# A hybrid decoder trunk on one core: the opening with another transfer order, engines in written order, and the second token half by feature tile

## The chip, the cores and the metric

One core of a Trainium2 chip runs the whole kernel in one launch. The metric is the device time in microseconds (us) of one execution, as the median of several. The core has five instruction queues that run beside each other, each in its own order: TensorE (PE, matmuls and transposes; its weight loads are shown apart as PEld), VectorE (DVE), ScalarE (ACT), GpSimd (POOL) and SyncE (SP, which here only issues transfers). Sixteen DMA engines move the data.

## What is computed

One layer with d = 1024 and 1024 tokens, all in float32. Only the opening and what feeds from it matter here:

```
mod = silu(c) @ ada_w + ada_b;  shift, scale, gate = split(mod, 3)
h = rms_norm(x, norm_w) * (1 + scale) + shift
proj = h @ w_in            # 10 slices: hq hf hi hz | gq gk gv gz ga | mg
y_h = hgrn2_branch(hq, hf, hi, hz);  y_g = gla_branch(gq, gk, gv, gz, ga)
merged = sigmoid(mg[0]) * (y_h @ w_branch[0]) + sigmoid(mg[1]) * (y_g @ w_branch[1])
out = rms_norm(x + gate * (merged @ w_out), final_norm_w)
```

Both branches are gated linear recurrences over the tokens, done in chunks ("attention" below).

## The kernel before

Features lie on the partitions: h is held as eight feature tiles of 128 rows by 1024 tokens. Each float32 operand of a large product is split into a rounded part hi and a rest lo, and a product is three matmuls: hi by hi, lo by hi and hi by lo. `split` does that: ACT casts hi (L192), DVE or POOL subtracts (L195).

The opening makes h and, with it, the first group of projections: six column tiles of w_in (gq, and half of gk; `NG = 6`), for each of two token halves of 512. Its steps, with their lines:

- `load_x` (L137) brings four token tiles of x, `norm_x` squares and sums them on ACT (L203), takes the root (L205) and scales on DVE (L206, L207). `transpose_x` turns 128 columns of four token tiles on PE (L214), and ACT copies the result out (L216).
- `load_mod` (L235) brings the shift and scale columns of ada_w for a block of one or two feature tiles, from all eight k tiles. `make_mod` weights and adds the k tiles on DVE (L246 the first, L250 the others), PE adds over the partitions with a column of ones (L258), DVE writes modv and amul (L260, L262). For block 0 the first four k tiles went through PE instead (L256). The blocks are `[(0, 1), (1, 1), (2, 2), (4, 2), (6, 2)]`: first tile, count.
- `make_h` applies modulation on ACT (L223), splits the result, and POOL stores h to memory (L226).
- `load_wg` (L280) brings 128 rows of w_in into one of three parts of the buffer xb, and `prep_wg` splits them, with POOL for lo.
- The products of the first half (L348) run feature tile by feature tile into six half banks, `accs`. `make_ga` (L304) makes the gate's low rank input, `qk_out` (L294, L296) copies the six results out.
- The second half: all eight tiles of h are made in a row, and `first_group` (L371) then goes column tile by column tile, each over all eight feature tiles, into new banks.

A small allocator, `Slots`, hands out 46 slots of 4 KB a partition, first freed first used; a new tile waits for all readers of the slot's last one. There are two banks for small PSUM tiles (`mtile`), taken in turn. Up to L323 (`order.close()`) PE, ACT and DVE keep the order of the program; behind it a list scheduler orders each engine by its own estimate. The rest of the program is a stream of jobs (features, blocks of values) into which `weave` puts the steps of side work, of which the decay `alpha_side` is the first.

Of the kernel before, what the change touches and what calls it, by code (L numbers as in the profile page):

```python
# [15 lines left out]
P = 128  # L16
D = 1024
T = 1024
# [64 lines left out]
def hybrid_trunk_kernel(  # L83
# [103 lines left out]
    def split(src, hi=None, lo=None, eng=None, pin=False):  # L187
# [4 lines left out]
        i = nc.scalar.copy(hi, src)  # L192
        if pin:
            tc.keep_in_program_order(i)
        (eng or nc.vector).tensor_sub(lo, src, hi.bitcast(F32))  # L195
        return hi, lo
# [23 lines left out]
    def make_h(half, d):  # L220
# [4 lines left out]
        if d % 2:  # L225
            nc.gpsimd.dma_start(h_d[half][d // 2], hT[half, d // 2].rearrange("p a t -> p (a t)"))  # L226

    def load_mod(d0, nd):
        kq = 4 // nd
        parts = []  # L230
        for kk in range(KT // kq):
# [5 lines left out]
            parts.append(b)  # L237
        return parts

    def make_mod(d0, nd, parts, on_pe):  # L240
        kq = 4 // nd
        acc = scT_f[:, (d0 // 2 % 2) * 512:(d0 // 2 % 2) * 512 + 2 * nd * P].rearrange("p (a f) -> p a f", a=2)
        for k in range(on_pe, KT):
            src = parts[k // kq][:, k % kq]
            if k == on_pe:
                i = nc.vector.tensor_scalar_mul(acc, src, cs[:, k:k + 1])  # L246
                if on_pe:
                    tc.keep_in_program_order(i)
            else:
                nc.vector.scalar_tensor_tensor(acc, src, cs[:, k:k + 1], acc, ALU.mult, ALU.add)  # L250
        pm = mtile()
        for half in range(2):
            for i in range(nd):
                o = pm[:, half * nd + i:half * nd + i + 1]
                for k in range(on_pe):
                    nc.tensor.matmul(o, parts[k // kq][:, k % kq, half, i * P:(i + 1) * P], cs[:, k:k + 1],  # L256
                                     start=(k == 0), stop=False)
                nc.tensor.matmul(o, acc[:, half, i * P:(i + 1) * P], one_t, start=(on_pe == 0), stop=True)  # L258
        S.free(*parts)
# [6 lines left out]
    NG = 6  # L266
# [10 lines left out]

    def load_wg(k):
        raw = xb_f[:, (k % 3) * 768:(k % 3) * 768 + 768]
        nc.sync.dma_start(raw, w_in[0, k * P:(k + 1) * P, C_GQ:C_GQ + NG * P])  # L280
        return raw

    def prep_wg(k, raw):
        split(raw[:, 0:512], wa_hi[k // 2][:, k % 2, :], wa_lo[k // 2][:, k % 2, :], nc.gpsimd, k < 2)
        split(raw[:, 512:768], wb_hi[k // 4][:, k % 4, :], wb_lo[k // 4][:, k % 4, :], nc.gpsimd, k < 2)
# [23 lines left out]
    blocks = [(0, 1), (1, 1), (2, 2), (4, 2), (6, 2)]  # L309
    mods, raws = {}, {}  # L310

    def load_mods(bi):
        mods[bi] = load_mod(*blocks[bi])

    def load_w(k):
        raws[k] = load_wg(k)

    for bi in range(3):
        load_mods(bi)
        load_w(bi)  # L320
    norm_x(0, x_t)
    vec_rows(rows_a, 24, R_SH)
    order.close()  # L323
    make_mod(0, 1, mods.pop(0), 4)
    transpose_x(0, x_t, 0)
    transpose_x(0, x_t, 1)
    acc0 = [dtile(), dtile()]
    accs = [acc0[f // 2][:, (f % 2) * 512:(f % 2) * 512 + 512] for f in range(4)]
    accs += [sc_ps[:, 0:512], sc_ps[:, 512:1024]]
    for bi, (d0, nd) in enumerate(blocks):  # L330
        if bi:
            make_mod(d0, nd, mods.pop(bi), 0)
        for d in range(d0, d0 + nd):
            make_h(0, d)
            prep_wg(d, raws.pop(d))
            if d + 3 < KT:
                load_w(d + 3)
            if d in (0, 2):
                load_mods(3 + d // 2)
            if d == 4:  # L340
                x_t2 = [load_x(t) for t in range(4, 8)]
            if d + 2 < KT:
                transpose_x(0, x_t, d + 2)
            if d == KT - 1:
                norm_x(1, x_t2)
            for f in range(NG):
                for n, (a, b) in enumerate(((0, h_hi), (1, h_hi), (0, h_lo))):
                    nc.tensor.matmul(accs[f], wg(a, d, f), b[d][:, 0:512],  # L348
                                     start=(d == 0 and n == 0), stop=(d == KT - 1 and n == 2))
    ga4, aw4 = S.get([T]), S.get([512])  # L350
    nc.gpsimd.memset(aw4, 0.0)
    for j in range(4):
        nc.gpsimd.dma_start(aw4[32 * j:32 * j + 16, :], alpha_w[0])
    make_ga(0)
# [4 lines left out]
    for d in range(KT):  # L359
        transpose_x(1, x_t2, d)  # L360
        make_h(1, d)

    def first_group():

        for f in range(NG):
            if f % 2 == 0:
                pd = dtile()
            ps = pd[:, (f % 2) * 512:(f % 2) * 512 + 512]
            for d in range(KT):
                for n, (a, b) in enumerate(((0, h_hi), (1, h_hi), (0, h_lo))):  # L370
                    nc.tensor.matmul(ps, wg(a, d, f), b[d][:, 512:1024],  # L371
                                     start=(d == 0 and n == 0), stop=(d == KT - 1 and n == 2))
                if d % 2:
                    yield
            qk_out(f, 1, ps)
# [1165 lines left out]
```

## Time and profile before

| what | value |
|---|---|
| median of 3 runs | 1249.74 us (1246.07 to 1254.04) |
| the profiled execution | 1252.38 us, its span 1250.7 us |
| busy: PE, DVE, ACT, POOL | 1205.7, 765.2, 530.4, 132.4 us |
| first product of the first half, end of the last | 24.81, 78.83 us |
| first product of the second half, first matmul of the next job (L454) | 83.77, 128.10 us |

Times in the rows below count from the start of the span. A row of the timeline gives start, length, engine, line, operation, out<-in, shape and count, and in brackets the idle time before it and what ended it. Lines are those of the kernel before.

### The profile page before, as it was taken

What the parts mean: (1) busy time and instruction counts of PE and PEld (TensorE: products, weight loads), DVE (VectorE), ACT (ScalarE), POOL (GpSimd) and SP (SyncE); (2) the same over time, 40 slices, a digit from 0 to 9 for tenths busy, and PEclk for the clock granted to TensorE, in tenths of its full rate; (3) what the DMA queues carried; (4) which work ended last, traced back from release to release, by engine and by line L of the source; (5) the groups of instructions that cost most, each with busy time, mean ns of one, the idle gap of its engine ahead of it and who ended that gap; (6) DMA issues with size and microseconds to landing.
All of it is one profiled execution on the core that took longest, in us unless ns stands there. A gap on an engine that the chain in (4) does not pass through costs nothing.

```text
span 1250.7 us, 20782 instructions
## 1 busy us (share of the span) xinstructions
PE 1205.7 (96%) x8603; PEld 999.9 (80%) x8603; DVE 765.2 (61%) x1219; ACT 530.4 (42%) x784; POOL 132.4 (11%) x216
## 2 busy tenths in 40 slices
PE   4799999999999999999999999999999999998997
PEld 3676899989798888788887878877888888787786
DVE  5746425494857556777873365695422668979443
ACT  4467713343334344243332323456643644454222
POOL 5510000201211021021110101011110000000000
PEclk9899999999999999999999999999999999999999
DMA  8832100653644167255251212154546556235202
GB/s 269 278 115 86 52 18 18 217 188 102 203 143 144 63 208 254 92 179 174 96 177 45 60 41 68 38 183 169 173 163 225 179 171 201 83 100 170 118 34 101
DMA packets 126928, 168.82 MB, mean 135 GB/s; under 512 B 7019, under 2 KB 97185, under 8 KB 126834
## 3 DMA queue, kind: packets, MB, share of 16 engines
q1 hardware_dynamic: 115234, 129.53, 33.5%
q0 software_dynamic: 11552, 37.97, 7.8%
q8 instruction: 67, 1.10, 0.4%
q14 instruction: 27, 0.22, 0.1%
q10 hardware_dynamic: 48, 0.01, 0.0%
HBM read 125.53 MB, written 41.94 MB: 134 GB/s over the span
## 4 chain that ended last, share of the span: by engine, by line
PE 59%; issue 24%; DVE 8%; DMA 3%; POOL 2%; ACT 2%; SPq 1%; POOLq 0%; DVEq 0%; ACTq 0%
PE pd L454 13%; PE pd L1313 11%; PE sc_ps L1313 5%; PE pm L1313 5%; PE pd L556 2%; PE pd L557 2%; PE pd L558 2%; DVE scT L250 1%; PE pm L761 1%; PE pm L742 1%; PE pm L763 1%; PE pd L1083 1%; PE pd L1084 1%; PE pd L1085 1%; DVE b L195 1%
## 5 line engine op out<-in xcount | busy, mean ns | idle before, releaser
L454 PE MATMUL pd<-b,b 128*128 128x512 f32 x1632 | 386.3, 393 | 0.0
L454 PEld LDWEIGHTS pd<-b,b 128*128 128x128 f32 x1632 | 302.4, 188 | 64.0 <-issue 0.5
L1313 PE MATMUL pd<-b,b 128*128 128x512 f32 x720 | 175.7, 395 | 2.5 <-DVE b L866 1.5
L1313 PEld LDWEIGHTS pd<-b,b 128*128 128x128 f32 x720 | 134.7, 189 | 35.4 <-DVE b L866 1.9
L195 DVE TENSOR_TENSOR b<-b,b 128x1024 fp32r<-128x1024 f32 (+1 forms) x95 | 101.8, 1082 | 74.7 <-ACT b L192 34.8
L192 ACT CAST b<-b 128x1024 fp32r<-128x1024 f32 (+1 forms) x95 | 84.6, 904 | 104.0 <-DVE b L1169 14.7
L1256 DVE TENSOR_TENSOR b<-b,b 128x1024 fp32r<-128x1024 f32 x56 | 68.3, 1224 | 68.5 <-ACT b L1255 46.6
L1255 ACT CAST b<-b 128x1024 fp32r<-128x1024 f32 x56 | 58.5, 1051 | 62.8 <-PE pd L1313 17.2
L1313 PE MATMUL sc_ps<-b,b 128*128 128x512 f32 x324 | 79.0, 391 | 0.3 <-ACT scT L706 0.3
L1313 PE MATMUL pm<-b,b 128*128 128x512 f32 x300 | 72.5, 389 | 3.4 <-DVE b L1256 3.4
L513 PE MATMUL pd<-b,b 128*128 128x256 f32 x256 | 74.2, 290 | 0.0
L515 PE MATMUL pd<-b,b 128*128 128x256 f32 x256 | 72.5, 283 | 0.0
L514 PE MATMUL pd<-b,b 128*128 128x256 f32 x256 | 72.4, 283 | 0.0
L1313 PEld LDWEIGHTS sc_ps<-b,b 128*128 128x128 f32 x324 | 60.4, 188 | 13.6 <-ACT scT L706 0.8
L1313 PEld LDWEIGHTS pm<-b,b 128*128 128x128 f32 x300 | 56.3, 188 | 15.5 <-DVE b L1256 3.8
L1234 DVE TENSOR_TENSOR b<-b,b 128x1024 fp32r<-128x1024 f32 x36 | 45.1, 1263 | 18.1 <-ACT b L1233 10.3
L1171 POOL DMA_DIRECT2D ws<-b x64 | 34.6, 541 | 194.8 <-DVE b L1165 87.1
L556 PE MATMUL pd<-b,b 128*128 128x512 f32 x128 | 52.0, 406 | 0.0
L557 PE MATMUL pd<-b,b 128*128 128x512 f32 x128 | 50.4, 394 | 0.0
L558 PE MATMUL pd<-b,b 128*128 128x512 f32 x128 | 50.4, 394 | 0.0
L648 ACT COPY xb<-b 128x512 f32<-128x512 f32 x48 | 29.5, 620 | 49.3 <-PE sc_ps L628 26.3
L1233 ACT CAST b<-b 128x1024 fp32r<-128x1024 f32 x36 | 37.2, 1049 | 28.9 <-PE pd L1313 10.1
(268 smaller groups left out, 2041.9 us busy)
## 6 DMA issues: line engine op xcount, KB each, us to landing
b<-in_w_in_dram SPq DMA_DIRECT2D x66, 512.0 KB, 4.0
ws<-b POOLq DMA_DIRECT2D x64, 256.0 KB, 3.0
b<-ws SPq DMA_DIRECT2D x32, 512.0 KB, 4.2
b<-in_x_dram SPq DMA_DIRECT2D x16, 512.0 KB, 5.8
b<-in_ada_w_dram SPq DMA_DIRECT2D x32, 256.0 KB, 6.2
b<-in_w_branch_dram SPq DMA_DIRECT2D x16, 512.0 KB, 4.8
b<-h SPq DMA_DIRECT2D x14, 512.0 KB, 4.2
b<-in_w_in_dram SPq DMA_DIRECT2D x24, 256.0 KB, 3.5
```

What stands on the lines that cost most here:

```text
L192: i = nc.scalar.copy(hi, src)
L195: (eng or nc.vector).tensor_sub(lo, src, hi.bitcast(F32))
L454: nc.tensor.matmul(ps[0:w, th * 512:(th + 1) * 512], a[:, k, 0:w], b[:, th * 512:(th + 1) * 512], start=(k == 0 and n == 0), stop=(k == KT ...
L513: nc.tensor.matmul(o, lh, hi[:, k % 4, :], start=(k == 0), stop=False)
L514: nc.tensor.matmul(o, lh, lo[:, k % 4, :], start=False, stop=False)
L515: nc.tensor.matmul(o, ll, hi[:, k % 4, :], start=False, stop=(k == KT - 1))
L556: nc.tensor.matmul(o, lh, hi[:, k % 2, :], start=(k == 0), stop=False)
L557: nc.tensor.matmul(o, lh, lo[:, k % 2, :], start=False, stop=False)
L558: nc.tensor.matmul(o, ll, hi[:, k % 2, :], start=False, stop=(k == KT - 1))
L1255: nc.scalar.copy(hi, t)
L1256: nc.vector.tensor_sub(lo, t, hi.bitcast(F32))
L1313: nc.tensor.matmul(o, a[:, sl], c, start=(p in (1, 5) and kt == 0 and n == 0), stop=(kt == 3 and n == 2), skip_group_check=True)
```

## The change

The code of the opening is written anew; what is computed stays the same.

- Transfers: block 0 of ada_w, then three row tiles of w_in in a row, then the next block, two more row tiles into slots of their own, and the third block. The blocks are cut as 1, 2, 2, 2, 1 tiles.
- Modulation: all k tiles go through DVE. `make_mod` is cut into `add_mod` and `end_mod`, and the sums of the next block are written between the steps of this one.
- The written order of PE, ACT and DVE now reaches to the first two transposes of the second half.
- The low part of the first row tile of w_in is made by DVE, of the others by POOL.
- h is stored by `store_h`, four stores in a row, behind each half.
- Products go hi by hi, then hi by lo of h, then lo by hi, each over the six column tiles, and `end_mod` stands ahead of the last six.
- The second half is made in `first_group`, feature tile by feature tile, into the same six half banks. `make_ga(1)` and the decay start at step 18 of 24, before at step 2.

```diff
-    def make_mod(d0, nd, parts, on_pe):
...
+    blocks = [(0, 1), (1, 2), (3, 2), (5, 2), (7, 1)]
...
+    def add_mod(bi, ks):
+        kq = 4 // blocks[bi][1]
+        acc = mod_acc(bi)
+        for k in ks:
+            src = mods[bi][k // kq][:, k % kq]
+            if k == 0:
+                nc.vector.tensor_scalar_mul(acc, src, cs[:, k:k + 1])
             else:
                 nc.vector.scalar_tensor_tensor(acc, src, cs[:, k:k + 1], acc, ALU.mult, ALU.add)
+
+    def end_mod(bi):
...
     def load_wg(k):
-        raw = xb_f[:, (k % 3) * 768:(k % 3) * 768 + 768]
...
+        if k in (3, 4):
+            raws[k] = S.get([T])
+        else:
+            raws[k] = xb_f[:, (k % 5 % 3) * 768:(k % 5 % 3) * 768 + 768]
...
-    order.close()
-    make_mod(0, 1, mods.pop(0), 4)
     transpose_x(0, x_t, 0)
-    transpose_x(0, x_t, 1)
+    add_mod(0, range(KT))
+    end_mod(0)
+    prep_wg(0, nc.vector)
+    x_t2 = []
     for bi, (d0, nd) in enumerate(blocks):
...
+        make_h(0, ds[0])
+        if more:
+            add_mod(bi + 1, range(2))
+            prep_wg(nxt[0], nc.gpsimd)
+        for d in ds[1:]:
             make_h(0, d)
...
+        if more:
+            add_mod(bi + 1, range(2, KT))
+        for d in nxt[1:]:
+            prep_wg(d, nc.gpsimd)
+        for d in ds[:-1]:
+            products(d, range(3))
+        for d in nxt:
+            transpose_x(0, x_t, d)
+        if more:
+            products(ds[-1], range(2))
+            end_mod(bi + 1)
+            products(ds[-1], (2,))
+        if bi == 0:
+            load_wg(5)
+            load_wg(6)
+            load_mod(3)
+            load_wg(7)
+            load_mod(4)
+        elif bi == 1:
+            x_t2.extend(load_x(t) for t in range(4, 8))
+    norm_x(1, x_t2)
+    products(KT - 1, (0,))
...
-    for d in range(KT):
+    for d in range(2):
         transpose_x(1, x_t2, d)
-        make_h(1, d)
+    order.close()
 
     def first_group():
 
-        for f in range(NG):
...
+        make_h(1, 0)
+        for d in range(KT):
+            if d + 2 < KT:
+                transpose_x(1, x_t2, d + 2)
+            if d + 1 < KT:
+                make_h(1, d + 1)
+            if d == KT - 2:
+                store_h(1)
+            for f in range(NG):
+                for n in range(3):
+                    product(1, d, f, n)
+                if d == KT - 1:
+                    qk_out(f, 1, accs[f])
+                if f % 2:
                     yield
-            qk_out(f, 1, ps)
```

Three places show what moves. The first is SP's queue in the opening (xb takes w_in's row tiles, b tiles from in_ada_w the modulation's columns). Before:

```order
L235 DMA b_177<-in_ada_w_dram 128x4x128 x2
L280 DMA xb<-in_w_in_dram 128x768
L235 DMA b_181<-in_ada_w_dram 128x4x128 x2
L235 DMA b_184<-in_ada_w_dram 128x4x128 x2
L280 DMA xb<-in_w_in_dram 128x768
L235 DMA b_188<-in_ada_w_dram 128x2x256 x2
```

In the changed kernel, where the same load of w_in is L291 and that of ada_w L239:

```order
L239 DMA b_179<-in_ada_w_dram 128x4x128 x2
L291 DMA xb<-in_w_in_dram 128x768 x3
L239 DMA b_185<-in_ada_w_dram 128x2x256 x2
L239 DMA b_188<-in_ada_w_dram 128x2x256 x2
L239 DMA b_191<-in_ada_w_dram 128x2x256 x2
L239 DMA b_194<-in_ada_w_dram 128x2x256 x2
L291 DMA b_197<-in_w_in_dram 128x768
L291 DMA b_199<-in_w_in_dram 128x768
```

The three row tiles fill xb at once, and the fourth and fifth (b_197, b_199) no longer go through xb.

The second place is DVE's queue around the modulation of feature tiles 4 to 7. Before, two blocks' sums stand ahead of the first block's modv (L260):

```order
L246 TENSOR_SCALAR scT<-b_371,cs 128x512
L250 SCALAR_TENSOR_TENSOR scT<-b_371,cs,scT 128x512
L250 SCALAR_TENSOR_TENSOR scT<-b_374,cs,scT 128x512 x2
L250 SCALAR_TENSOR_TENSOR scT<-b_377,cs,scT 128x512 x2
L250 SCALAR_TENSOR_TENSOR scT<-b_380,cs,scT 128x512 x2
L260 TENSOR_TENSOR modv<-pm_449,vec 128x2x2
L262 SCALAR_TENSOR_TENSOR amul<-modv,vec 128x2
L260 TENSOR_TENSOR modv<-pm_537,vec 128x2x2
```

In the changed kernel L253 and L255 are the sums, L266 and L268 modv and amul, and L193 the low part of h:

```order
L255 SCALAR_TENSOR_TENSOR scT<-b_322,cs,scT 128x512 x2
L255 SCALAR_TENSOR_TENSOR scT<-b_325,cs,scT 128x512 x2
L255 SCALAR_TENSOR_TENSOR scT<-b_328,cs,scT 128x512 x2
L266 TENSOR_TENSOR modv<-pm_489,vec 128x2x2
L268 SCALAR_TENSOR_TENSOR amul<-modv,vec 128x2
L193 TENSOR_TENSOR b_153<-b_384,b_145 128x512
L253 TENSOR_SCALAR scT<-b_332,cs 128x256
L255 SCALAR_TENSOR_TENSOR scT<-b_332,cs,scT 128x256
L193 TENSOR_TENSOR b_154<-b_470,b_146 128x512
```

Each block's modv stands behind its own sums alone, and h's low parts between the next ones.

The third place is ACT's queue between the two halves (b_416 to b_422 hold the second half of x, pm_619 is the bank of `make_ga`, b_758 holds the raw weights of the first feature job). In the changed kernel L201 squares, L319 copies the gate, L214 copies a transpose:

```order
L192 CAST b_147<-b_470 128x512
L201 ACTIVATE b_570,ssx<-b_416 128x1024
L203 ACTIVATE rsx<-ssx,eps_t 128x1
L201 ACTIVATE b_575,ssx<-b_418 128x1024
L203 ACTIVATE rsx<-ssx,eps_t 128x1
L201 ACTIVATE b_580,ssx<-b_420 128x1024
L203 ACTIVATE rsx<-ssx,eps_t 128x1
L201 ACTIVATE b_585,ssx<-b_422 128x1024
L203 ACTIVATE rsx<-ssx,eps_t 128x1
L192 CAST b_806<-b_758 128x1024
L319 COPY b_608<-pm_619 128x512
L214 COPY b_642<-pm_643 128x512
```

Before, at the same place:

```order
L203 ACTIVATE b_592,ssx<-b_470 128x1024
L205 ACTIVATE rsx<-ssx,eps_t 128x1 x2
L306 COPY b_615<-pm_622 128x512
L216 COPY b_645<-pm_646 128x512
L223 ACTIVATE b_645<-b_645,modv,amul 128x512
```

The cast of the first feature's weights now stands ahead of the gate's copy. Their load is SP's next instruction behind x, into the slot that b_585, the output of the fourth square, had. On DVE the MEMSET of pm_619 (L313) stands behind the four scalings of x, where before the MEMSET of pm_622 (L300) stood ahead of them.

More of the change, by code (lines that the diff above doesn't have):

```diff
@@ L224, in make_h, with store_h, load_mod @@
         split(b, h_hi[d][:, sl], h_lo[d][:, sl])
[L225 to L228 removed]
+    def store_h(half):
+        for i in range(4):
+            nc.gpsimd.dma_start(h_d[half][i], hT[half, i].rearrange("p a t -> p (a t)"))
+    blocks = [(0, 1), (1, 2), (3, 2), (5, 2), (7, 1)]
+    mods = {}
+    def load_mod(bi):
+        d0, nd = blocks[bi]
         kq = 4 // nd
[L230 removed]
+        mods[bi] = []
         for kk in range(KT // kq):
@@ L253, in make_mod @@
             for i in range(nd):
[L254 to L259, printed above, removed]
+                nc.tensor.matmul(pm[:, half * nd + i:half * nd + i + 1], acc[:, half, i * P:(i + 1) * P], one_t,
+                                 start=True, stop=True)
+        S.free(*mods.pop(bi))
         nc.vector.tensor_add(modv[:, :, d0:d0 + nd], pm[:, 0:2 * nd].rearrange("p (a b) -> p a b", a=2),
@@ L350, in hybrid_trunk_kernel @@
+    norm_x(1, x_t2)
+    products(KT - 1, (0,))
+    for f in range(NG):
+        for n in (1, 2):
+            product(0, KT - 1, f, n)
     ga4, aw4 = S.get([T]), S.get([512])
```

98 lines of the change are left out of this document (40 added, 58 removed).

## The prediction

> **What bounds the kernel now.** I read the page first, then the windows, then the timeline of single engines through the opening.
>
> The page:
> ```profile
> span 1250.7 us, 20782 instructions
> PE 1205.7 (96%) x8603; PEld 999.9 (80%) x8603; DVE 765.2 (61%) x1219; ACT 530.4 (42%) x784; POOL 132.4 (11%) x216
> ```
> TensorE is busy for 96%, so the kernel is as long as TensorE's work and its 45 us of idleness. The windows tell where these lie (columns: stretch, length, busy time of PE, PEld, DVE, ACT and POOL with instruction counts, granted clock, DMA share, GB/s):
> ```profile
> 0.00:20.00 20.00, 6.98 (x30) 6.05 (x30) 6.02 (x15) 9.01 (x17) 13.42 (x55) 1.00 0.97 289
> 20.00:40.00 20.00, 12.88 (x50) 9.29 (x50) 17.82 (x28) 9.74 (x19) 8.98 (x9) 0.92 0.80 260
> 40.00:60.00 20.00, 16.47 (x73) 13.45 (x72) 13.02 (x17) 7.15 (x15) 9.61 (x10) 0.84 0.88 295
> 60.00:80.00 20.00, 20.00 (x88) 15.59 (x92) 10.48 (x21) 8.81 (x20) 5.08 (x8) 0.90 0.17 61
> ```
> PE is idle for 13.0 + 7.1 + 3.5 = 23.7 us before 60 and not at all in the next 20. The change can win no more than that and what the lowered clock costs. The first token half's products stand in PE's timeline as L348, the second half's as L371 (start, length, engine, line, operation, count):
> ```profile
> 24.81 1.22 PE L348 MATMUL pd<-b,b 128*128 128x512 f32 x2 [1.62 <-ACT b L192]
> 26.26 4.25 PE L348 MATMUL pd<-b,b 128*128 128x512 f32 x10
> 30.34 1.32 PE L348 MATMUL sc_ps<-b,b 128*128 128x512 f32 x5
> 38.21 1.22 PE L348 MATMUL pd<-b,b 128*128 128x512 f32 x2 [1.20 <-ACT b L192]
> 51.87 1.53 PE L348 MATMUL sc_ps<-b,b 128*128 128x512 f32 x6
> 60.61 2.05 PE L348 MATMUL pd<-b,b 128*128 128x512 f32 x4
> 74.59 2.88 PE L348 MATMUL pd<-b,b 128*128 128x512 f32 x12
> 77.31 1.52 PE L348 MATMUL sc_ps<-b,b 128*128 128x512 f32 x6
> 83.77 1.66 PE L371 MATMUL pd<-b,b 128*128 128x512 f32 x6
> ```
> Feature tile 0's 18 products take 24.8 to 31.7, tile 1's start at 38.2, tiles 2 and 3 end at 53.4, tiles 4 to 7 run without a pause from 60.6 to 78.8. A product costs 2.72/12 = 0.227 us at full clock (74.59 to 77.31) and 0.425 us at half clock (26.26, x10). The pauses before 38.2 and 60.6 are waits for modulation: DVE sums eight k tiles of ada_w, PE adds over partitions, and then ACT can make h.
>
> **Part 1: the transfers.**
> ```profile
> 20.63 6.81 SPq L280 DMA_DIRECT2D xb<-in_w_in_dram x2
> 32.01 9.07 SPq L280 DMA_DIRECT2D xb<-in_w_in_dram x2
> 21.00:24.00 3.00, 1.12 (x4) 0.71 (x4) 2.54 (x8) 1.56 (x3) 0.00 (x0) 1.00 1.10 351
> 39.00:42.00 3.00, 3.00 (x8) 1.93 (x7) 2.96 (x3) 3.00 (x7) 2.23 (x4) 0.50 0.23 21
> ```
> SP stands still for 6.8 and 9.1 us until a third of xb is free, and the rate falls from 351 to 21 GB/s. With the new order no load waits for a reader that is late: x, ada_w and the six feature columns of w_in are 2.1 + 8.4 + 3.1 = 13.6 MB; 289 GB/s to 20 us bring 5.8 MB, and 351 GB/s the other 7.8 MB in 22 us, so the last lands near 43 to 45, and x's second half near 53. The sums below need each tile later than that, so DMA stops being a limit and is worth nothing more by itself.
>
> **Part 2: the chain of modulation.** Its links, beside the sums:
> ```profile
> 14.72 1.52 DVE L250 SCALAR_TENSOR_TENSOR scT<-b,cs,scT 128x256 f32<-128x256 f32 x3
> 51.67 4.69 DVE L250 SCALAR_TENSOR_TENSOR scT<-b,cs,scT 128x512 f32<-128x512 f32 x6 [0.19 <-DMA b<-in_ada_w_dram]
> 24.98 5.20 DVE L250 SCALAR_TENSOR_TENSOR scT<-b,cs,scT 128x256 f32<-128x256 f32 x4
> 24.90 2.17 POOL L195 TENSOR_TENSOR b<-xb,b 128x512 fp32r<-128x512 f32 x2 [10.43 <-ACT b L192]
> 27.45 2.17 POOL L195 TENSOR_TENSOR b<-xb,b 128x512 fp32r<-128x512 f32 x2 [0.38 <-ACT b L192]
> 24.38 0.68 DVE L195 TENSOR_TENSOR b<-b,b 128x512 fp32r<-128x512 f32 x1
> 53.24 0.95 PE L258 MATMUL pm<-ones,scT 128*128 128x1 f32 x8
> 57.54 0.81 ACT L223 ACTIVATE b<-b,modv,amul 128x512 f32<-128x512 f32 x1 [0.51 <-DVE amul L262]
> 58.73 0.62 ACT L192 CAST b<-b 128x512 fp32r<-128x512 f32 x1
> 59.96 0.57 ACT L216 COPY b<-pm 128x512 f32<-128x512 f32 x1
> 11.66 0.75 DVE L207 TENSOR_SCALAR b<-b,rsx 128x1024 f32<-128x1024 f32 x1
> ```
> A sum costs 0.51 us at 256 columns and 0.78 at 512; four 256 column sums took 5.20 instead of 2.03 us while POOL subtracted for 4.3 us. So DVE and POOL hold each other up: up to 3.2/4.3 = 0.7 us of DVE per us of POOL. The change leaves this in: POOL makes the low parts of w_in for tiles 1 to 7, 2.2 us each, while DVE sums.
>
> Start: x is normalised at 12.4 (11.66 + 0.75). Block 0 (tile 0 alone) now has all eight sums on DVE: 0.35 + 7 x 0.51 = 3.9, to 16.4; PE's four small products and DVE's two small writes end at 17.5; L223 and L192 (0.8 + 0.6 us) give the first product at 19.1 instead of 24.8 (some 12 at half clock, as before). Leaving L256 out of PE costs nothing, PE has nothing else there.
>
> Then the written order makes a cycle, from one block's modulation to the next: h 1.5, its low part 0.7, the eight sums 6.0 (0.49 + 7 x 0.78), the second tile's low part 0.7, PE's sum 1.0 (L258 x8), modv and amul 0.4: 10.3 us, plus what POOL holds back. Two tiles are 4.4 us of POOL, beside DVE for only part of it: between 0 and 3.2, and I take 1.8. So 12.1 us a block of two. PE needs 36 x 0.227 + 1.0 for two tiles' transposes + 1.0 = 10.2 us for the same block: DVE's chain sets the pace and PE waits some 2 us a block. Modulation is ready at 17.5, 28.6 (block 1, one low part less), 40.6, 52.6 and 62.4 (eight narrow sums, but PE is still busy with tiles 5 and 6); tile 7's 18 products run from 64.1 to **68.1, against 78.8: 10.7 us won**. With no hold at all it would be 64.3, with the full one 68.5.
>
> **Part 3: between the halves.** Until now tiles 4 to 7 hid the norm of the second x. Now nothing does:
> ```profile
> 4.79 1.04 ACT L203 ACTIVATE b<-b 128x1024 f32<-128x1024 f32 x1
> 6.21 1.04 ACT L203 ACTIVATE b<-b 128x1024 f32<-128x1024 f32 x1
> 61.24 0.48 DVE L300 MEMSET pm<- 128x512 f32 x1
> 78.76 1.91 PE L304 MATMUL pm<-b,wga 128*16 128x512 f32 x16
> b<-in_w_in_dram SPq DMA_DIRECT2D x6, 512.0 KB, 3.9
> ```
> ACT squares four tiles behind tile 7's cast: 64.0 + 4 x 1.4 (6.21 - 4.79) = 69.6. DVE's last multiply ends at 70.6, and only behind it in order stands the MEMSET of the gate's bank: PE starts L304 at 71.2 instead of 68.1. ACT's next instruction is now the cast of the first feature's weights. Their load goes into the slot of the fourth square's output, so it is issued near 69.3 and lands 3.9 us later (the last row, median of x6), at 73.3; the cast (1.05 us) holds the gate copy to 75.0 and the copies of the transposes behind it. h of tile 0 is there at 77.6, so the second half's products start at 77.7 with three, and steadily at 78.8: 78.4 on the mean, with L304 and four tiles' transposes done. Before, the same state was reached at 83.77. **Of 10.7 us, 5.4 are left.**
>
> **Part 4: the clock.**
> ```profile
> 36.00:39.00 3.00, 1.80 (x11) 1.39 (x10) 2.92 (x6) 2.73 (x6) 1.34 (x2) 0.62 0.74 294
> 57.00:60.00 3.00, 1.27 (x8) 1.12 (x6) 0.50 (x1) 2.49 (x6) 2.86 (x4) 0.54 0.74 302
> 56.49 0.66 PE L214 MATMUL pm<-ident,b 128*128 128x128 f32 x4 [1.80 <-DVE modv L260]
> 58.88 1.87 PE L258 MATMUL pm<-ones,scT 128*128 128x1 f32 x8 [1.73 <-ACT b L216]
> ```
> Twice, after some 7 us without dense products, the granted clock is halved, for about 6.8 us, and comes back in dense work. Between 68.1 and 78.8 PE has 4 of 10.7 us of work, so I count a third such drop: some 12 products at 0.425 instead of 0.227 us, **2.4 us lost** (none to 3.4 by what 6.8 us at half speed can cost). The drops at 36.8 and 57 go, and are in the 10.7. The Trainium skill, "TensorE: Matmul & The Clock Gate", section "HAM oscillation — how this bites in real kernels", asks only for no idle gap over about 3.4 us. Here the drop of 57 came with idle gaps of 1.80 and 1.73 us, so the trace speaks against it as a safe bound.
>
> **Part 5: what else moves.** In the second half, tile by tile, ACT needs 0.57 + 0.81 + 0.62 = 2.0 us a tile (L216, L223, L192) and PE 18 x 0.227 + 0.5 = 4.6: covered, at nothing; with the cover gone PE would wait for ACT. The products go into the banks of the first half; DVE's six copies out of them, some 0.7 us each from 71.1 on, end before 77.7. The decay's side work (from the 18th step of the first group instead of the 2nd) is needed by the first attention, which starts behind two more features and a block of values: hidden. POOL issues the same eight stores of h, and their readers come hundreds of us later. On SP the load of the fourth feature stands ahead of the second's and waits for a slot that is free when tile 3 of the second half is done, near 98; the second's weights then land some 8 us later, near 106, and PE wants them a feature behind the first group's end, near 130. So all of this is 0, between -2 and 2 us. Behind the first group PE's rows stand nearly as before, and the longest wait there is
> ```profile
> PE pm L1313 <- DVE b L1256: 3.4, 1, 3.4
> ```
> One such wait less or more is -3 to 3 us; I take 0.
>
> **Sum.** -10.7 + 5.3 + 2.4 + 0 + 0 = -3.0 us. The profiled execution took 1252.38 (span 1250.7), 2.64 over the median of the runs shown, 1249.74. From the median: **1246.7 us**. 1% of it, about what can be told from no change, is 12.5 us.
>
> **Rivals.**
> *The clock holds in the gap* (0.20). PE has L304 and 16 transposes there, no gap over 3.1 us. Then -5.4: 1244.3. This is also what the Trainium skill's 3.4 us (same page) would give; the row at 57 speaks against it.
> *DVE is held less than assumed, and the clock holds* (0.08). 512 column sums take long in one piece, and POOL's two subtractions could slip between. Half 0 ends at 64.3 and the gap moves with it: -5.4 - 3.8 = -9.2, 1240.5, and a little lower if the load lands sooner.
> *The clock drops in each block's wait* (0.17). PE waits 1 to 3 us a block, with its thin sums beside. With a drop of 6.8 us in each of three blocks half 0 ends at 76 to 79 and the second half starts near 86: +2, and its first products are slow too: +4, 1254.
> *The clock never rises in the opening: slower* (0.10). Place: the products of tiles 0 to 7. Price: 0.2 us each. At 0.425 a block of two is 36 x 0.425 + 2 + 1.2 = 18.5 us on PE, over the 12.1 of the chain, and PE becomes the bound: half 0 ends near 90, the second half starts near 96 instead of 83.8, and with its own slow start that is +14.5: 1264. It decides from some 27 slow products on the bound path (5.4/0.2). Against it: the clock rose in each dense stretch of 7 us, and the new ones are 7 to 11 us long.
> *The opening's gain doesn't reach the end* (0.05): a later wait for DVE, such as L1313's, takes it. 1249.7.
> The forecast has 0.40, by itself 1243 to 1250.
>
> **Range and chances.** 1240 to 1257 leaves out the never rising clock and about half of the second rival. Faster by over 1% (under 1237.2): 0.05, from the second rival's low end. Slower by over 1% (over 1262.2): 0.10. Within: 0.85.
>
> **What would show it.** In the new profile: first product near 19; no SP stall on xb before 30; products of tiles 1, 3, 5 and 7 starting near 30, 42, 54 and 64, each behind amul; sums of 1.25 us where POOL subtracts; a PE gap from 68 to 78 ended by DVE's MEMSET and ACT's cast; a clock near 0.5 around 80. It is wrong if sums beside POOL take 0.5 and 0.8, if the weights' load lands before the squares end, or if PE's idle time after 200 us differs by more than 3 us.

## The result, and the profile after

| kernel | median | runs | ratio to before | 95% interval |
|---|---|---|---|---|
| before | 1249.66 us (1246.07 to 1254.04) | 9 | 1 | |
| changed | 1255.28 us (1252.03 to 1259.10) | 9 | 1.0050 | 1.0031 to 1.0069 |

The change makes the kernel slower by 0.5%, some 5.6 us. The forecast was 1246.7 us, 3.0 us faster: the sign is wrong, the time lies inside the range of 1240 to 1257. The profiled execution of the changed kernel took 1256.71 us.

The page of the changed kernel, span and engines:

```profile
span 1255.0 us, 20765 instructions
PE 1205.5 (96%) x8587; PEld 1000.8 (80%) x8587; DVE 775.9 (62%) x1225; ACT 534.6 (43%) x785; POOL 132.2 (11%) x214
```

PE is busy as long as before (1205.5 against 1205.7 us). So the 4.3 us by which this span is longer are idle time of PE. In both kernels a part of PE's busy time is work at a lowered clock. The windows of the opening (stretch, length, busy time of PE, PEld, DVE, ACT and POOL, granted clock, DMA share, GB/s):

```profile
0.00:20.00 20.00, 5.71 (x19) 3.99 (x20) 9.73 (x24) 12.02 (x23) 15.45 (x55) 1.00 0.93 293
20.00:40.00 20.00, 15.45 (x59) 12.45 (x59) 16.00 (x18) 7.58 (x15) 10.55 (x9) 0.83 1.08 367
40.00:60.00 20.00, 17.09 (x75) 13.45 (x74) 14.02 (x20) 7.74 (x15) 6.32 (x7) 0.86 0.55 187
60.00:80.00 20.00, 16.74 (x79) 11.39 (x78) 13.59 (x27) 9.81 (x20) 5.85 (x9) 0.93 0.24 85
```

The transfers do what they were to do: 367 GB/s between 20 and 40 us, 260 before, and little left behind 60. But PE's idle time of 23.7 us before 60 has only become 21.8, there is a new one behind 60, and the granted clock is again below full in three of the four windows. PE's timeline through the opening (start, length, engine, line, operation, count, idle time before it; L263 is the sum over the partitions, L328 the products of both halves, L317 the gate's products, L212 the transposes):

```profile
19.51 2.08 PE L328 MATMUL pd<-b,b 128*128 128x512 f32 x4 [0.20 <-ACT b L192]
28.95 1.83 PE L263 MATMUL pm<-ones,scT 128*128 128x1 f32 x8 [4.55 <-DVE scT L255]
42.98 1.02 PE L263 MATMUL pm<-ones,scT 128*128 128x1 f32 x8 [1.52 <-DVE scT L255]
56.21 1.02 PE L263 MATMUL pm<-ones,scT 128*128 128x1 f32 x8 [1.39 <-DVE scT L255]
73.39 1.07 PE L328 MATMUL sc_ps<-b,b 128*128 128x512 f32 x4
77.19 2.71 PE L317 MATMUL pm<-b,wga 128*16 128x512 f32 x16 [2.73 <-issue]
83.46 0.73 PE L328 MATMUL pd<-b,b 128*128 128x512 f32 x2
```

The first product starts at 19.51 instead of 24.81, and the first half ends at 74.46 (73.39 + 1.07) instead of 78.83: 4.4 us won, not 10.7. The second half starts at 83.46 against 83.77: of the 4.4 us, 0.3 are left.

Then the rest. PE alone in four windows, of the changed kernel:

```profile
84.00:128.00 44.00, 44.00 (x202) 1.00 0.37 120
128.00:400.00 272.00, 271.49 (x2438) 1.00 0.34 111
400.00:600.00 200.00, 192.80 (x1712) 0.98 0.44 143
600.00:830.00 230.00, 230.00 (x2035) 0.99 0.34 110
```

Between 400 and 600 us PE is idle for 7.2 us, in the kernel before for 1.2 (the row is from the second profile of it, below). In the other three stretches the kernel before is idle for 4.4 us and the changed one for 0.5, so that PE idles some 2 us more on balance up to 830 us. Its waits in the whole execution (engine, what it waited for: us in total, times, longest):

```profile
PE pm L783 <- ACT b L762: 3.9, 2, 3.4
PE pm L1354 <- DVE b L1297: 3.4, 1, 3.4
PE sc_ps L669 <- DVE tot L672: 2.8, 1, 2.8
PE pm L317 <- issue: 2.7, 1, 2.7
```

The second row is the wait that the prediction quoted of before (there L1313 on L1256). The first and the third are new; both belong to an attention, one at 587, one at 470 us. How they come about is seen in DVE's and ACT's timelines just ahead of them. DVE:

```profile
459.84 0.69 DVE L1207 TENSOR_TENSOR b<-b,b 128x512 f32<-128x512 f32 x1 [4.58 <-DMA b<-in_w_in_dram]
463.67 0.69 DVE L1206 TENSOR_TENSOR b<-b 128x512 f32<-128x512 f32 x1 [1.81 <-DMA b<-in_w_in_dram]
469.27 0.38 DVE L672 TENSOR_TENSOR tot<-tot 128x64 f32<-128x64 f32 x1
```

and ACT:

```profile
581.26 1.05 ACT L192 CAST b<-b 128x1024 fp32r<-128x1024 f32 x1 [6.17 <-DMA ws<-b]
582.21 1.04 ACT L629 COPY xb<-b 128x1024 f32<-128x1024 f32 x1
586.53 0.97 ACT L762 COPY b<-pm 128x512 f32<-128x512 f32 x2
```

L1206 and L1207 are sums of weights for the last stages (`weight_sums`, which `prepare` runs as side work: load two blocks of weights, add them, store the sums as ws). In DVE's order they stand ahead of the attention's multiplications up to L672, and they wait 4.58 and 1.81 us for their own loads. At 581 a cast of the next feature's weights waits 6.17 us, for a slot out of which a store of such sums still reads, and the attention's copies up to L762 stand behind the cast. PE then waits for L672 and L762.

### The profile page after: what moved, and what is told of

Same layout as the page of the kernel before. It is cut to its first block, busy times and chain, and to the rows that moved or that the text cites. A ratio compares the mean times of both kernels' runs of the same rounds, so it can differ in the third digit from the quotient of the medians.

```text
span 1255.0 us, 20765 instructions
## 1 busy us (share of the span) xinstructions
PE 1205.5 (96%) x8587; PEld 1000.8 (80%) x8587; DVE 775.9 (62%) x1225; ACT 534.6 (43%) x785; POOL 132.2 (11%) x214
## 4 chain that ended last, share of the span: by engine, by line
PE 42%; issue 8%; DVE 1%; DMA 1%; POOL 1%; ACT 1%; SPq 0%; POOLq 0%; ACTq 0%; DVEq 0%
PE pd L1354 11%; PE pd L495 8%; PE sc_ps L1354 5%; PE pm L1354 5%; PE pd L597 1%; PE pd L599 1%; PE pd L598 1%; PE pd L1124 1%; PE pd L1125 1%; PE pd L1126 1%; PE pm L783 1%; DMA b<-in_w_out_dram 1%; PE pm L1126 1%; PE pm L1124 1%; PE pm L1125 1%
## 5 line engine op out<-in xcount | busy, mean ns | idle before, releaser
L495 PE MATMUL pd<-b,b 128*128 128x512 f32 x1632 | 389.4, 395 | 0.0
L1354 PE MATMUL pd<-b,b 128*128 128x512 f32 x720 | 176.3, 396 | 2.3 <-DVE b L907 1.5
L1354 PEld LDWEIGHTS pd<-b,b 128*128 128x128 f32 x720 | 135.2, 190 | 35.2 <-DVE b L907 1.9
L193 DVE TENSOR_TENSOR b<-b,b 128x1024 fp32r<-128x1024 f32 (+1 forms) x95 | 104.2, 1106 | 65.4 <-ACT b L192 48.6
L192 ACT CAST b<-b 128x1024 fp32r<-128x1024 f32 (+2 forms) x99 | 86.4, 888 | 117.1 <-DMA b<-in_w_in_dram 15.5
L1296 ACT CAST b<-b 128x1024 fp32r<-128x1024 f32 x56 | 58.5, 1050 | 60.5 <-PE pd L1354 17.3
L1354 PE MATMUL sc_ps<-b,b 128*128 128x512 f32 x324 | 79.0, 391 | 0.3 <-ACT scT L747 0.3
L1354 PE MATMUL pm<-b,b 128*128 128x512 f32 x300 | 72.9, 391 | 3.9 <-DVE b L1297 3.4
L1354 PEld LDWEIGHTS sc_ps<-b,b 128*128 128x128 f32 x324 | 60.4, 188 | 13.6 <-ACT scT L747 0.7
L1354 PEld LDWEIGHTS pm<-b,b 128*128 128x128 f32 x300 | 56.3, 188 | 16.5 <-DVE b L1297 3.8
L328 PE MATMUL pd<-b,b 128*128 128x512 f32 x192 | 57.1, 434 | 0.7 <-ACT b L192 0.7
L597 PE MATMUL pd<-b,b 128*128 128x512 f32 x128 | 51.1, 399 | 0.0
L599 PE MATMUL pd<-b,b 128*128 128x512 f32 x128 | 49.9, 390 | 0.0
L598 PE MATMUL pd<-b,b 128*128 128x512 f32 x128 | 49.8, 389 | 0.0
```

The source lines that it names most:

```text
L495: nc.tensor.matmul(ps[0:w, th * 512:(th + 1) * 512], a[:, k, 0:w], b[:, th * 512:(th + 1) * 512], start=(k == 0 and n == 0), stop=(k == KT ...
L597: nc.tensor.matmul(o, lh, hi[:, k % 2, :], start=(k == 0), stop=False)
L598: nc.tensor.matmul(o, lh, lo[:, k % 2, :], start=False, stop=False)
L599: nc.tensor.matmul(o, ll, hi[:, k % 2, :], start=False, stop=(k == KT - 1))
L1296: nc.scalar.copy(hi, t)
L1354: nc.tensor.matmul(o, a[:, sl], c, start=(p in (1, 5) and kt == 0 and n == 0), stop=(kt == 3 and n == 2), skip_group_check=True)
```

## The experiments

The new waits lie 400 us behind the changed code, so the first question was how the change reaches there. `weave` puts one step of side work behind so many steps of the main stream. Counted from the code, in these steps:

| | before | changed |
|---|---|---|
| `alpha_side`, first and last step | 3, 38 | 19, 54 |
| first attention | 57 | 60 |
| second load of the side track `prepare` | 106 | 129 |
| last step of `prepare` | 310 | 353 |

The decay ends 16 steps later. Its last pause (6, counted down by 1.1 a step) keeps the attention, which is next on the same track, until step 60; the attention's values have been ready since step 56. That moves the attentions by 3 steps, and with them the times at which slots are free. `prepare` goes on only where 12 slots are free, just misses one such time, and comes 23 to 43 steps late. **Theory A**: this, and not the opening itself, makes the loss. **Theory B**: the state in which the new opening hands over engines and slots makes it.

Two places in the trace serve as marks for all kernels: the first product of the second half, and the first product of the last stages (L1313, changed L1354). The work of PE between them is nearly the same in all kernels; `first_half_only` is left out of that comparison, since its first product starts ahead of a wait.

### Only the later decay

```diff
 # kernel before
-                if i == 2:
+                if i == 18:
                     make_ga(1)
                     start_side(alpha_side())
```

> The kernel before with one number changed: alpha_side starts at step 18 of the first group instead of step 2, as it must in the changed kernel. By the code this alone puts every later side step where the changed kernel has it: alpha ends at step 54 instead of 38, the first attention starts at 60 instead of 57, and the blocks' weight sums (prepare) end at 353 instead of 310, because they find too few free slots more often. Theory A (the place of the side steps makes the loss of the changed kernel behind 400 us): PE's waits near 470 us (on DVE's tot) and near 587 us (on ACT's copy of the transposed keys) are there, those of before at 268 and 329 us are not, and the kernel is slower than before by 4 to 8 us, 1254 to 1258 us. Theory B (the loss comes from the phase in which the new opening hands over its engines, slots and queues, or from a slower opening): within 2 us of before, 1248 to 1252 us, without these two waits.

Measured (`late_alpha`): 1255.75 us, ratio 1.0061 (1.0046 to 1.0077). PE's two waits in its timeline:

```profile
470.53 0.89 PE L628 MATMUL sc_ps<-xb,b 128*32 128x48 f32 x64 [2.68 <-DVE tot L631]
587.39 3.35 PE L742 MATMUL pm<-b,b 128*128 128x128 f32 x14 [4.44 <-ACT b L721]
```

They are the two of the changed kernel, in a kernel with the old opening and the old second half. A holds, and B is not needed for these waits: this one number alone, 6.4 us by the medians, costs as much as the whole change. That does not yet say that the rest of the change is free.

### The changed kernel with the side work at its old steps

```diff
 # changed kernel, alpha_side
                 S.free(zb)
-            yield 6
+            yield 6 if h0 == 0 else 2
```

> The changed kernel with one number changed: the last pause of alpha_side is 2 steps instead of 6. Alpha still starts at step 18, but by the code the first attention is back at step 57, and all later side steps stand where they stood before (weight sums end at 310 again). Theory A: the waits near 470 and 587 us go, before's at 268 and 329 us come back (1.4 us each), and the opening and second half keep what they win over before by 128 us (2.6 us): 1247 us (1245 to 1249.5). Theory B: as the changed kernel, 1253 to 1257 us.

Measured (`alpha_short`): 1251.85 us, ratio 1.0027 (1.0016 to 1.0037). The waits at 470 and 587 are gone and two at 265 and 326 are back, as A says, and 3.4 us come back. But the time lies 2.4 us over A's range, and it is clearly slower than before. Its second half starts in the profile at 82.17 us, and before in a second profile (below) at 82.61: the opening has won hardly anything that could be left over, and A had counted 2.6 us. Where the other 2.5 us over before lie, the profiles cannot show: the profiled execution took 1250.68 us, and the two of before 1250.78 on the mean. So the rest of the change costs some 2.5 us beside the side steps, and its place is open.

### The new first half alone

```diff
 # changed kernel
-    for d in range(2):
-        transpose_x(1, x_t2, d)
     order.close()
+    for d in range(KT):
+        transpose_x(1, x_t2, d)
+        make_h(1, d)
+    store_h(1)
...
-                if i == 18:
+                if i == 2:
```

(and `first_group` as before, column tile by column tile).

> The changed kernel with its second half undone: the first token half with the new transfers and written orders, then all eight transposes and make_h and the second half's products column by column in banks of their own, alpha at step 2, the written order closed ahead of the transposes. The side steps stand as in before. Theory A: the new first half breaks even at the start of the second half's products (about 83.5 against 83.8 us), the second half costs what it cost before, and the rest is as before: 1249.5 us (1247.5 to 1251.5). Theory B: the new first half's hand-over makes the later waits: 1253 to 1257 us.

Measured (`first_half_only`): 1251.49 us, ratio 1.0023 (1.0012 to 1.0034), the upper end of A's range. Without the tile by tile half the late decay isn't needed, and the two waits are gone. But the interval lies above 1: the new first half does not break even, as A had it, but costs 2.2 us by the medians.

### POOL's subtractions to DVE

```diff
 # changed kernel, loop over the blocks
-            prep_wg(nxt[0], nc.gpsimd)
+            prep_wg(nxt[0], nc.vector)
...
-            prep_wg(d, nc.gpsimd)
+            prep_wg(d, nc.vector)
```

> The changed kernel, with the low parts of the first group's weights (prep_wg) subtracted by DVE instead of POOL in every block of the first half. In the changed kernel four POOL subtractions (5.0 us a block) stand beside DVE, and DVE's instructions there take 1.53 (L253), 1.11 (L255) and 1.78 us (L193) instead of 0.49, 0.78 and 0.69. Theory A (POOL's subtractions hold DVE, 3.0 us a block): these go back to 0.49, 0.78 and 0.69, DVE gets 2 x (0.69 + 0.42) = 2.2 us of subtractions instead, so a block's cycle falls from 13.2 to about 12.4 us and the first half ends near 72 instead of 74.4 us; the total falls by 0 to 3 us, as the gap behind the first half may take it back. Rival: DVE is slow there for another reason (its operands, the PSUM banks), so the durations stay and the cycle grows by the 2.2 us to about 15.4 us; the first half ends near 80 us.

Measured (`dve_lo`): 1248.46 us, ratio 1.0004 (0.9990 to 1.0018): by the medians 6.8 us less than the changed kernel, by the ratios 5.7. The same block in both timelines, first the changed kernel (POOL, then DVE: sum of k tile 0, of k tile 1, low part of the second h, the other six sums, modv):

```profile
33.35 5.00 POOL L193 TENSOR_TENSOR b<-b,b 128x512 fp32r<-128x512 f32 x4 [0.38 <-ACT b L192]
33.38 1.53 DVE L253 TENSOR_SCALAR scT<-b,cs 128x512 f32<-128x512 f32 x1
34.95 1.11 DVE L255 SCALAR_TENSOR_TENSOR scT<-b,cs,scT 128x512 f32<-128x512 f32 x1
35.98 1.78 DVE L193 TENSOR_TENSOR b<-b,b 128x512 fp32r<-128x512 f32 x1
37.68 5.15 DVE L255 SCALAR_TENSOR_TENSOR scT<-b,cs,scT 128x512 f32<-128x512 f32 x6
44.04 0.17 DVE L266 TENSOR_TENSOR modv<-pm,vec 128x4 f32<-128x4 f32 x1 [1.21 <-PE pm L263]
```

and without POOL:

```profile
30.99 0.48 DVE L253 TENSOR_SCALAR scT<-b,cs 128x512 f32<-128x512 f32 x1
31.50 0.75 DVE L255 SCALAR_TENSOR_TENSOR scT<-b,cs,scT 128x512 f32<-128x512 f32 x1
32.17 1.62 DVE L193 TENSOR_TENSOR b<-b,b 128x512 fp32r<-128x512 f32 x3
33.71 4.68 DVE L255 SCALAR_TENSOR_TENSOR scT<-b,cs,scT 128x512 f32<-128x512 f32 x6
38.31 1.02 DVE L193 TENSOR_TENSOR b<-b,b 128x512 fp32r<-128x512 f32 x2
39.75 0.17 DVE L266 TENSOR_TENSOR modv<-pm,vec 128x4 f32<-128x4 f32 x1 [0.41 <-PE pm L263]
```

Modulation comes every 11.3 us (28.42 to 39.75) instead of every 13.2 (30.82 to 44.04), though DVE now does 2.0 us of subtractions itself (1.62 + 1.02 less 0.6 for h). Row by row, POOL's 5.0 us a block held DVE for 3.0 us: 1.53 - 0.48, 1.11 - 0.75, 1.78 - 0.69 and 5.15 - 4.68. Of DVE's own 2.0 us only the first 1.0 delays modulation; the rest runs while PE sums over the partitions, for which DVE now waits 0.41 instead of 1.21 us. So the cycle should be 13.2 - 3.0 + 1.0 = 11.2 us, which is what came. The first half ends at 67.2, the second starts at 76.0, 7.4 us earlier than in the changed kernel, and most of this reaches the end, though the waits at 464 (2.76 us) and 580 (2.07) are there. My own expectation (a cycle of 12.4 us, 0 to 3 us won) had the hold right, but counted all of DVE's own subtractions as delay, and the gap behind the first half took nothing back.

The Trainium skill, "SBUF — State Buffer", section "SBUF: two separate sides", says that DVE and GpSimd share one pair of ports, and that a GpSimd instruction, or a DVE one that needs the pair (in a 2-port mode, or with two SBUF inputs while GpSimd reads SBUF), holds it alone for its whole length, while the other is blocked. The rows agree: next to POOL's four subtractions (1.25 us each) DVE's instructions take 1.11 to 1.78 instead of 0.48 to 0.75 us. L253, with one tensor as its input, is held too; whether it runs in a 2-port mode no trace shows.

### Both edits, and the norm moved

`both` is the edits of `alpha_short` and `dve_lo` together. `three` adds this:

```diff
 # norm_x: ACT's squares and roots only; DVE's part becomes scale_x
+        if bi == 3:
+            norm_x(1, x_t2)
         for d in nxt:
             transpose_x(0, x_t, d)
...
-    norm_x(1, x_t2)
+    for i, xt in enumerate(x_t2):
+        scale_x(1, i, xt)
     products(KT - 1, (0,))
```

> The changed kernel with two edits together: the low parts of the first group's weights by DVE instead of POOL, and the last pause of alpha_side 2 steps instead of 6, so that the side steps stand as in the kernel before. If the two costs add up (A): the 6.8 us of the first edit and the 3.4 us of the second, 1255.3 - 6.8 - 3.4 = 1245 us (1243 to 1247). If the waits behind 400 us only move with the phase of the engines (B), the second edit brings nothing here: 1248 to 1250 us.

> The last kernel with a third edit: ACT's four squares of the second half's x stand in the fourth block (ahead of the transposes of tile 7), and DVE's four scalings behind tile 7's low part, so that the transposes of the second half can follow tile 7's products at once. In the kernel with the low parts by DVE alone, tile 7's products end at 67.2 us and the second half's begin at 76.0. Theory: this gap of 8.8 us is made by the squares, by the scalings behind them and by the first feature's weights, whose load waits for the fourth square's slot; with the squares early, the gap is 4 to 5.5 us (the gate's products 1.0, two tiles' transposes 1.0, their copies, h and its low part 2 to 3), and the kernel gains 3 to 5 us: 1240 to 1242. Rival: x lands too late (53 us) or ACT has no room in the fourth block, so that tile 7's h comes later by what the gap gets shorter: within 1 us of the kernel with two edits.

Measured: `both` 1246.65 us, ratio 0.9964 (0.9951 to 0.9977); `three` 1243.56 us, ratio **0.9941 (0.9928 to 0.9954)**, faster than both kernels of the case. By the ratios the two edits should give 1.0050 - 0.0046 - 0.0023 = 0.9981; they give somewhat more. So they add up (A). The profiles are less exact than this: `both` and `dve_lo` have the same opening, and their second halves start at 78.63 and 76.03 us. `three` lies 1.6 us over the 1240 to 1242 that were expected of it, and 3.1 us under `both`, so its rival falls.

PE's timeline of `three` between the halves (products L334, gate L323):

```profile
66.60 1.07 PE L334 MATMUL sc_ps<-b,b 128*128 128x512 f32 x4
68.05 1.91 PE L323 MATMUL pm<-b,wga 128*16 128x512 f32 x16 [0.39 <-PE sc_ps L334]
72.56 0.66 PE L218 MATMUL pm<-ident,b 128*128 128x128 f32 x4 [0.66 <-ACT b L220]
73.08 0.73 PE L334 MATMUL pd<-b,b 128*128 128x512 f32 x2
```

5.4 us from the end of the first half to the second, against 9.0 in the changed kernel: the squares, the scalings and the late weights, which this edit moves together, made 3.6 us of the gap. In the windows of `three` the granted clock is full from 40 to 80 us, where the changed kernel had 0.86 and 0.93 (and `both` 1.00 and 0.91):

```profile
40.00:60.00 20.00, 18.83 (x90) 14.89 (x91) 15.20 (x30) 13.58 (x26) 2.79 (x6) 1.00 0.63 211
60.00:80.00 20.00, 18.23 (x95) 13.08 (x95) 12.17 (x23) 11.31 (x20) 3.36 (x6) 1.00 0.32 112
```

### Second profiles

> The kernel before, profiled a second time. Its first profile, the one the prediction was worked out on, is of an execution of 1252.38 us, 3.0 us over the median of 27 runs (1249.34). Reading C: that execution lost its 3 us in the opening (a late load of x, or one drop of the granted clock more), so that a new profile near the median starts the second half's products 1 to 3 us before 83.77 us and has the same work behind it; the new opening then loses to the usual one. Reading D: it lost them behind 128 us, in the drop at 661 us and the waits at 268, 329 and 831 us; a new profile then starts the second half within 0.7 us of 83.77 us and is shorter behind it.

> The changed kernel, profiled a second time. Theory A (the order of the side work makes the two waits): the waits of PE near 470 us on DVE's tot (2.8 us) and near 587 us on ACT's copy (3.4 us) are there again within 0.5 us, since they stand in the order and not in the run; a time of 1253 to 1258 us. Against it: one of them is gone, and then it was of that execution alone.

Before, again: 1249.18 us, and a profile of it:

```profile
82.61 1.65 PE L371 MATMUL pd<-b,b 128*128 128x512 f32 x6
326.75 0.89 PE L628 MATMUL sc_ps<-xb,b 128*32 128x48 f32 x64 [1.37 <-DVE tot L631]
821.46 1.52 PE L1313 MATMUL pd<-b,b 128*128 128x512 f32 x6
...
400.00:600.00 200.00, 198.77 (x1754) 1.00 0.50 160
```

Its second half starts 1.2 us earlier than in the profile the prediction was made on, and the stretch to the last stages is 3.1 us shorter: each reading holds in part, D for the larger part. Changed, again: 1256.12 us, PE waits 3.39 us at 469.5 and 3.52 at 587.0, the first of them 0.6 us longer than in the first profile, where 0.5 was allowed. So these two waits stand in the order of the instructions. And against the second profile of before (82.61), the changed opening (83.46 and 82.64) wins nothing.

### Which side work?

```diff
 # kernel before (sums_late)
-    stream.back.append([prepare(), 60])
+    stream.back.append([prepare(), 96])
 # changed kernel (sums_early), twice
-            while len(S.free_list) < 12:
+            while len(S.free_list) < 11:
```

> The kernel before with one number changed: the track of the weight sums (prepare) waits 96 steps instead of 60. By the code alpha (3 to 38) and the attentions (from 57) stay where they are, but the first loads fall at step 96 instead of 94, the second finds too few free slots and falls at 129 instead of 106, and the track ends at 353 instead of 310, as in the changed kernel. Of theory A this tells apart which steps make the waits. A1 (the later weight sums: their additions stand in DVE's order ahead of an attention's and wait there for their loads): the waits of PE near 470 and 587 us appear, and the kernel is 4 to 7 us slower than before. A2 (the attentions' 3 steps): within 1.5 us of before, no such waits.

> The changed kernel with one number changed: the side track asks for 11 free slots instead of 12 before it goes on. By the code alpha (19 to 54) and the attentions (from 60) stay as in the changed kernel, but the weight sums end at step 302 instead of 353 (310 in the kernel before). A1 (the later weight sums make the waits): the waits near 470 and 587 us go, and the time falls by 3 to 6 us, to 1249 to 1252 us. A2 (the attentions' 3 steps): as the changed kernel, 1254 to 1257 us.

Measured: `sums_late` 1254.38 us, ratio 1.0033 (1.0021 to 1.0045); `sums_early` 1255.55 us, 1.0043 (1.0028 to 1.0059). PE's longest new waits, first of `sums_late`, then of `sums_early`:

```profile
328.97 0.89 PE L628 MATMUL sc_ps<-xb,b 128*32 128x48 f32 x64 [2.81 <-DVE tot L631]
```

```profile
401.50 1.32 PE L669 MATMUL sc_ps<-xb,b 128*32 128x48 f32 x64 [2.50 <-DVE tot L672]
```

Late sums alone cost 4 us, so A2 falls; but the wait is at 329, not at 470 and 587 as A1 had it. Early sums leave 1.02 us of the wait at 470 (at 474) and 0.80 us of that at 587, and make one at 401; the time is the one A2 gave, and nothing is won, against A1. So neither track alone is the cause. The rows fit a cause in how the steps of the two tracks lie to each other and to the stream. Which of the arrangements are good was not settled. The marks show it for all kernels:

| kernel | side steps | second half starts | last stages start | between | to the end |
|---|---|---|---|---|---|
| before | old | 83.77 | 825.71 | 741.9 | 425.0 |
| before, again | old | 82.61 | 821.46 | 738.9 | 426.0 |
| `alpha_short` | old | 82.17 | 822.52 | 740.4 | 426.4 |
| `both` | old | 78.63 | 819.59 | 741.0 | 426.9 |
| `three` | old | 73.08 | 812.93 | 739.9 | 427.0 |
| changed | changed | 83.46 | 827.58 | 744.1 | 427.4 |
| changed, again | changed | 82.64 | 827.37 | 744.7 | 427.1 |
| `late_alpha` | changed | 82.14 | 827.75 | 745.6 | 425.8 |
| `dve_lo` | changed | 76.03 | 819.04 | 743.0 | 429.7 |
| `sums_late` | sums late | 82.94 | 827.38 | 744.4 | 425.4 |
| `sums_early` | sums early | 83.62 | 828.37 | 744.8 | 426.0 |

With the old steps the stretch between takes 738.9 to 741.9 us, with any others 743.0 to 745.6: 4.0 us more on the mean, whatever the opening. The last column is 425.5 us on the mean of the two profiles of before and 427.2 on those of the changed kernel, 1.7 more, which no run here explains. It looks tied to the new opening rather than to the side steps: this column is 425.0 to 426.0 us in the four profiles with the old opening and 426.0 to 429.7 in the others.

## Why the prediction was wrong, step by step

- **Part 1, transfers: right.** No load of w_in waits for a third of xb any more, and DMA is no limit behind 45 us.
- **Part 2, first product: right.** 19.51 against 19.1 us.
- **Part 2, the cycle of a block: mis-sized.** The term "between 0 and 3.2, and I take 1.8" for what POOL holds back measured 3.0 us a block. The bound held; the reason for taking less, that POOL is "beside DVE for only part of it", failed: POOL's four subtractions, 5.0 instead of 4.4 us, stand beside a working DVE from the first to the last (33.35 to 38.35). Not only the sums are held, but also the one input TENSOR_SCALAR (1.53 instead of 0.48 us) and the subtractions. Modulation came at 30.8, 44.0, 57.3 and 68.1 instead of 28.6, 40.6, 52.6 and 62.4. The hold is the 1.2 us by which the cycles of 13.2 are longer than 12.0. Block 1 lost 1 us more, mainly in PE's sum (1.83 instead of 1.0 us, at half clock), and the last block 1 us, where PE itself was the bound and had 3.4 us at half clock. So the first half won 4.4 us instead of 10.7. The end given for the full hold, 68.5, was summed wrongly besides: 1.4 us more in three blocks is 4.2 us, which gives 72.3.
- **Part 3, the gap between the halves: right.** From the end of the first half to the first product of the second 9.6 us were forecast, 9.0 measured, with the same steps: MEMSET, gate's products, the weights' load issued behind the fourth square, their cast, the gate copy.
- **Part 4, the clock: the drop right, its price too high.** The drop in the gap came, at 78.1, but PE had mainly the gate's products (2.71 instead of 1.91 us) and transposes in it: about 1 us, not 2.4. In exchange the rival "the clock drops in each block's wait" (0.17) came true in the first half: drops at 26.9, 44.0 and 57.7, shorter than assumed (6.8, 3.4 and 3.4 us).
- At this point the sum should have been -3.0 us. In the profiles it was 0: -0.3 against the first one of before, and between 0 and +0.9 against the second. By the medians it was a loss: with the side steps at their old places the change costs 2.5 us (`alpha_short`), its first half alone 2.2 (`first_half_only`), and what of this lies behind the opening is open.
- **Part 5, "hidden": a term put at nothing that cost 3.4 us.** This is the difference between the changed kernel and `alpha_short`; in the kernel before the same shift cost 6.4 us (`late_alpha`). I set the later decay at nothing because the first attention starts behind two more features and a block of values. I compared when it is needed in time, and not in the steps by which the code places it: its pause ends at 60, the values are there at 56. Beside that I had not asked who is placed behind it: all later attentions and, over the free slots, the weight sums. A sign of being wrong that the prediction names came true here: between 200 and 1240 us PE is idle for 12.8 and 12.2 us in the two profiles of before, and for 16.3 and 16.9 in those of the changed kernel. The rest of Part 5 held where it was looked at: in the second half PE is busy for 44.0 of 44 us.
- **"One such wait less or more is -3 to 3 us; I take 0."** Two longer waits came, with a drop of the clock at each, and two shorter ones went: +4.0 us in the stretch to the last stages, about half of it idle time and the rest slower work, and +1.7 behind it, whose cause is open. In the profiles that is the 5.6 us of the medians. The rival "the opening's gain doesn't reach the end" (0.05) had the right kind of place, but as the end of a gain, not as a loss of its own.

## What to carry to other kernels

Where code places side work by counting steps or free slots, a start moved by some steps is a change of the whole program behind it: count where each later step lands before costing it at nothing. A hold between two engines is priced for all the work that stands beside the holder, and taken at less only where rows show that the two miss each other. And a gain of 3 us is within what two profiles of one kernel differ by here (3.2 us), so that a forecast of this size needs more than one profile of before.

## What the runs showed of the hardware that was not expected

The granted clock falls behind waits that are much shorter in one place than in another. Windows of PE, of the changed kernel (stretch, length, PE busy, granted clock, DMA share, GB/s):

```profile
44.00:47.40 3.40, 3.40 (x10) 0.50 1.03 402
57.70:61.10 3.40, 3.40 (x9) 0.50 0.34 139
470.70:474.10 3.40, 3.40 (x9) 0.50 0.83 222
834.00:837.40 3.40, 3.40 (x17) 1.00 0.40 154
```

PE's waits of 1.52 and 1.39 us, which ended at 43.0 and 56.2, were each followed by 1.0 us of one column products and then by 3.4 us at half clock. The wait of 2.80 us that ended at 469.7 was followed by a drop too. A wait of 1.46 us that ended at 833.4, in dense work, was not. Nor was the wait of 2.68 us of `late_alpha` at 470.5 (clock 1.00 from 470 to 476), while one of 2.07 us of `dve_lo` at 580.0 was (0.50 from 582 to 584). So the length of the wait alone does not decide. The Trainium skill, "TensorE: Matmul & The Clock Gate", section "HAM oscillation — how this bites in real kernels", wants no idle gaps over about 3.4 us; here 1.4 to 1.5 us were enough in the opening. That thinner work around the wait makes the difference fits the opening's rows (17.09 of 20 us busy from 40 to 60), but no run tested it by itself. At half clock a product costs 0.2 us more (0.425 instead of 0.227), so a drop of 3.4 us costs PE some 1.7 us where it is the bound, on top of the wait.
